# Loading a side job's first weights before the last projection, with rooms of their own and waits by tile

## The chip, the cores and the metric

The kernel runs on one NeuronCore of a Trainium2 chip. The metric is the device time of one execution in microseconds; of several runs the median counts. The profile comes from one further execution that was recorded; its times count from the start of its span.

## What is computed

One layer of a streaming encoder, on 1024 tokens of width 1024: a mixer with two groups of heads, a cross attention to 256 memory tokens, and an MLP, each added to its input.

```python
h = h + parallel_mixer(rms_norm(h, norm_mix_g), w_in, ..., w_out)
h = h + memory_cross_attention(rms_norm(h, norm_xattn_g), rms_norm(mem, norm_mem_g), xattn_wq, xattn_wkv, ..., xattn_wo)
u = relu(rms_norm(h, norm_mlp_g) @ mlp_w1)
h = h + (u * u) @ mlp_w2
```

Inside the mixer `proj = xn @ w_in` is split into queries, keys and values of 8 "forgetting attention" (FoX) heads and of 4 heads of gated linear attention (GLA). The two head groups' outputs stand side by side, and `w_out` projects them: rows 0 to 511 of `w_out` belong to FoX, rows 512 to 1023 to GLA. Memory keys and values are `memn @ wkv`; the keys are normalized and multiplied by the norm vectors.

## The kernel before

Every float32 product is made of three matmuls on split operands: each operand is a high part (rounded) and a low part (the rest), and `gemm` (lines 110 to 112) adds high·high, high·low and low·high. Splitting costs one instruction on ScalarE (the high part) and one on VectorE (the low part) for each tile of 128 x 512. `wsplit` does so for weights: it loads two blocks of 128 rows at a time into a tile `raw` (512 KB, line 80), and makes `wh` (line 88 or 99) and `wl` (line 93 or 100) of each block. There are nine rooms for such pairs; a tenth pair waits until the matmuls that read the first have ended. The `raw` tiles come by turns from a pool `rawp` with two rooms and, where `rooms` is given, from two rooms called `raw0` in that pool.

The order of the work on each engine is fixed when the program is built: a scheduler with a model of the durations places each instruction, and the engine then runs its own list in that order, waiting where an operand is not ready. ScalarE, VectorE and the queue of DMA issues on SyncE (SP) thus each hold up all that stands behind a waiting instruction. A memory room that a pool takes over from an earlier pool makes its first users wait for the last users of what lay there.

`mixer_inputs` computes the projections. Its last stages are, for each of 8 blocks of 128 tokens, the GLA output, and then the projection of the FoX values with W_FV: eight products of 24 matmuls (`token_major`), each evicted from PSUM by a pair on ScalarE and VectorE into a staging tile `qn` (lines 120 and 121), and written to DRAM as `vd` (line 596). While that runs, `fox_prep` loads queries and keys of the first heads (lines 636 to 642) and `fox_group` makes the first scores (lines 656 to 659), their maximum `nm` (661), exponential `p` (664) and normalization (667, on GpSimd).

Then comes `fox`: for each of 8 heads it loads the values `va` of all token blocks from `vd` (line 721), transposes `p` (`tr`, line 696), splits it (`pth`, `ptl`), and multiplies by the values (`pv`, lines 703 and 704). `va` needs all eight writes of `vd`. Between these steps a generator, `side_work`, is advanced: it first loads the norm vectors `gx` and `gxk` (lines 739 to 741), then runs `out_part`: it splits rows 512 to 1023 of `w_out` (the first 512 columns) with `wsplit`, splits the GLA outputs `mixg` into `sh` and `sl` (lines 832, 833), multiplies, adds `x` (`t2k`, lines 805, 806) and writes `hpd` (807). After that it loads `memT` and `mem` into `memr` (749, 754), and projects the memory with four slices of `wkv`. All tiles of the side work come from one pool `side`, which lies where `mixer_inputs` had its normalized input (`xn`: tiles `xh0`, `xl0` for tokens 0 to 511, `xh1`, `xl1` for the others); it waits for that pool as a whole, and so does every pool of `fox`.

Of the kernel before, what the change touches and what calls it, by code (L numbers as in the profile page):

```python
# [17 lines left out]
F32 = mybir.dt.float32  # L18
F32R = mybir.dt.float32r
# [3 lines left out]
ALU = mybir.AluOpType  # L23
AX = mybir.AxisListType
PSUM = bass.MemoryType.PSUM
# [3 lines left out]
D = 1024  # L29
M = 256  # L30
P = 128
KT = D // P
NT = S // P
# [18 lines left out]
class Layer:  # L52
# [11 lines left out]
        return pool.tile(shape, dt, tag=tag, name=f"{tag}_{self.n}", **kw)  # L64


    def wsplit(self, src, gcols, N=512, lo_pool=0, hi_pool=False, steps=None, beside=None, rooms=None, nraw=2):


        nc = self.nc  # L70
        kt = src.shape[0] // P
        hs, ls = [], []
        for k0, n in steps or [(k, 2) for k in range(0, kt, 2)]:
            if beside is not None:
                beside(k0, n)
            self.nr += 1
            raw = (self.T(self.rawp, [P, 2, N], F32, "raw") if rooms is None or nraw == 2 and self.nr % 2
                   else self.T(rooms, [P, 2, N], F32, "raw0", bufs=nraw))
            eng = nc.scalar if beside is not None and k0 == 0 else nc.sync
            self.raw_load = eng.dma_start(raw[:, 0:n], src[k0 * P:(k0 + n) * P, :].rearrange("(k p) n -> p k n", p=P))  # L80
            for j in range(n):
                wp = self.wps[self.nw % len(self.wps)]
                self.nw += 1
                wh = self.T(wp, [P, N], F32R, "wh")
                wl = self.T(wp, [P, N], F32R, "wl")
                r = raw[:, j, :]
                if gcols is None:
                    nc.scalar.activation(wh, r, AF.Copy)
                    if lo_pool and (k0 + j) % lo_pool == 0:
                        for c in (slice(0, N // 2), slice(N // 2, N)):  # L90
                            nc.gpsimd.tensor_tensor(wl[:, c], r[:, c], f(wh[:, c]), ALU.subtract)
                    else:
                        nc.vector.tensor_tensor(wl, r, f(wh), ALU.subtract)
                else:
                    g = self.cols[:, gcols + k0 + j:gcols + k0 + j + 1]
                    if hi_pool:
                        nc.gpsimd.tensor_scalar(wh, r, g, 1.0, ALU.mult, ALU.mult)
                    else:
                        nc.scalar.activation(wh, r, AF.Identity, scale=g)
                    nc.vector.scalar_tensor_tensor(wl, r, g, f(wh), ALU.mult, ALU.subtract)  # L100
                hs.append(wh)
                ls.append(wl)
        return hs, ls
# [94 lines left out]
    def build(self):  # L198
        with ExitStack() as st:
            dram = self.open(st, "dram", space=DRAM)  # L200
            self.qd = self.T(dram, [8, 2, 64, S], F32, "qd")
            self.kd = self.T(dram, [8, 2, 64, S], F32, "kd")
            self.vd = self.T(dram, [P, 8, NT, P], F32, "vd")
            self.cq = self.T(dram, [8, 4, S], F32, "cq")
            self.ck = self.T(dram, [8, 4, S], F32, "ck")
            self.kTd = self.T(dram, [P, 2, KT, M], F32, "kTd")
            self.vmd = self.T(dram, [P, 2, 2, D], F32, "vmd")
            self.od = self.T(dram, [P, 2, 2, KT, 512], F32, "od")
            self.hpd = self.T(dram, [2, KT, P, 512], F32, "hpd")
            self.hd = self.T(dram, [P, KT, S], F32, "hd")  # L210
            self.fd = self.T(dram, [P, 2, 512], F32, "fd")
            self.ud = self.T(dram, [NQ, P, 8, 512], F32, "ud")
            self.consts(self.open(st, "const"))
            self.smallp = self.open(st, "small", 6)
            ws = st.enter_context(ExitStack())
            self.rawp = self.open(ws, "raw", 2)
            self.wps, self.nw = [self.open(ws, "w", 9)], 0
            lst = st.enter_context(ExitStack())
            with ExitStack() as mx:
                self.mixg = self.T(self.open(mx, "mixg"), [P, NT, 4, P], F32, "mixg")  # L220
                with ExitStack() as mm:
                    self.mm_stack = mm
                    self.mixer_inputs()
                    self.side = self.open(mx, "side")
                    self.mixf = self.T(self.open(mx, "mixf"), [P, NT, 4, P], F32, "mixf")
                    self.fox()

                self.mmp = self.open(lst, "mm3", 2, space=PSUM)
                self.trp = self.open(lst, "tr3", 2, space=PSUM)

                self.h = self.T(self.open(st, "h", side="right"), [P, KT, S], F32, "h")
                self.project_out()
            self.xattn()
# [38 lines left out]
    def mixer_inputs(self):  # L272
        nc = self.nc
        w_in = self.w_in
        with ExitStack() as st:
            xnp = self.open(st, "xn")
            xh, xl = [], []
            for i in range(2):
                xh.append(self.T(xnp, [P, KT, 512], F32R, f"xh{i}"))
                xl.append(self.T(xnp, [P, KT, 512], F32R, f"xl{i}"))  # L280
            stp = self.open(st, "stg", 2)
            trp = self.trp = self.open(st, "tr1", 2, space=PSUM)
            mst, gst = ExitStack(), ExitStack()
            mmp = self.open(mst, "mm1", 3, space=PSUM)
# [39 lines left out]
            with ExitStack() as s2:  # L324
# [14 lines left out]
                def factors(t):  # L339
# [10 lines left out]
                                steps=[(0, 1), (1, 1), (2, 2), (4, 2), (6, 2)], beside=columns(0), rooms=xp, nraw=5)  # L350
# [138 lines left out]
            beside = decays()  # L489
# [98 lines left out]
            self.fox_first = self.fox_prep(0)  # L588
            self.fox_p = self.fox_group(0, 0, self.fox_first)
            W = self.wsplit(w_in[:, W_FV:W_FV + 512], C_MIX)  # L590
            for t in range(NT):
                ps = token_major(t, W)
                vv = self.T(stp, [P, 8, 2, 64], F32R, "qn")
                v3 = ps.rearrange("p (h d) -> p h d", h=8)
                self.evac_split(vv[:, :, 0, :], vv[:, :, 1, :], v3, self.xr[:, t:t + 1])
                nc.sync.dma_start(self.vd[:, :, t, :], f(vv).rearrange("p h s d -> p h (s d)"))
# [22 lines left out]


    def fox_open(self):
        self.foxp = self.open(self.mm_stack, "fox", 2, side="right")
        self.fox3 = self.open(self.mm_stack, "fox3", 3, side="right")
        self.fox_s = self.open(self.mm_stack, "sps", 1, space=PSUM, side="right")
# [49 lines left out]
    def fox(self):  # L674
        nc = self.nc
        with ExitStack() as st:
            pt = self.open(st, "foxpt", 5)
            olp = self.open(st, "foxol", 3)
            mmp = self.open(st, "mm2", 1, space=PSUM)
            pvp = self.open(st, "pv2", 1, space=PSUM)  # L680
            trp = self.open(st, "tr2", 3, space=PSUM)

            def values(h, sb, pp, A):
                va = A[4]
# [45 lines left out]
            for _ in side:  # L730
                pass

    def side_work(self, mp, mmp, trp):


        nc = self.nc
        v2 = lambda ap: ap.rearrange("p (h d) -> p h d", h=2)
        gk = self.T(mp, [P, 256], F32, "gxk")
        nc.sync.dma_start(self.gx, self.xq_g.partition_broadcast(P))
        nc.sync.dma_start(gk, self.xk_g.partition_broadcast(P))  # L740
        nc.vector.scalar_tensor_tensor(self.gx, self.gx, 0.0625, gk, ALU.mult, ALU.mult)
        yield from self.out_part(mp, mmp, 0, ())

        mh, ml = ([self.T(mp, [P, 4, P], F32R, n, bufs=6) for _ in range(4)] for n in ("sh", "sl"))
        gm = self.cols[:, C_MEM:C_MEM + 8]
        for t in range(2):
            c1 = slice(t, t + 1)
            xt = self.T(mp, [P, 4, M], F32, "memr")
            nc.sync.dma_start(xt, self.memT[:, 4 * t:4 * t + 4, :])
            for j in range(4):  # L750
                k, c = 4 * t + j, slice(2 * (j % 2), 2 * (j % 2) + 2)
                self.evac_split(mh[k // 2][:, c, :], ml[k // 2][:, c, :], xt[:, j, :].rearrange("p (t s) -> p t s", t=2), gm[:, k:k + 1])
            xt = self.T(mp, [P, D], F32, "memr")
# [3 lines left out]
            nc.gpsimd.tensor_tensor(self.mr[:, c1], self.mv[:, c1], self.mhalf[:, 0:1], ALU.pow)  # L757
            yield
        for n in range(4):
            W = self.wsplit(self.wkv[:, n * 512:(n + 1) * 512], None, rooms=mp)  # L760
            for t in range(2):
                ps = self.T(mmp, [P, 512], F32, "mm")
                self.gemm(ps, *([m[k // 2][:, 2 * (k % 2) + t, :] for k in range(KT)] for m in (mh, ml)), *W)
                kv = self.T(mp, [P, 2, 512], F32R, "mkv", bufs=2)
# [23 lines left out]
    def out_part(self, mp, mmp, n, ks):  # L788
# [1 line left out]

        nc = self.nc
        cs = slice(n * 512, (n + 1) * 512)
        W = self.wsplit(self.w_out[512:1024, cs], None, rooms=mp)
        if ks:
            W = [a + b for a, b in zip(W, self.wsplit(self.w_out[ks[0] * P:(ks[-1] + 1) * P, cs], None, rooms=mp))]
        for half in range(2):
            A = self.split_half(mp, self.mixg, half, 6, range(4))
            if ks:
# [546 lines left out]
```

## Time and profile before

| | |
|---|---|
| time, median of 3 runs | 1450.64 us (1450.14 to 1451.19) |
| time of the profiled execution | 1454.34 us |
| its span | 1452.6 us |
| mean granted TensorE clock | 0.996 |
| TensorE matmul busy | 1427.7 us (98%) |
| VectorE busy | 948.6 us (65%) |
| ScalarE busy | 679.9 us (47%) |
| GpSimd busy | 397.1 us (27%) |

The time of an execution is the span and about 1.7 us around it. The last matmul of the value projection starts at 326.62 us; `fox` with its side work fills the time from there to about 559 us. In rows of a timeline the first number is the start, the second the duration, both in microseconds; what stands in brackets is how long the engine was idle before and which engine and operation ended that. "PEclk" in a table of windows is the clock that TensorE was granted, as a share of full speed.

### The profile page before, as it was taken

To read this page: it belongs to the slowest core of one execution; us is meant where nothing else is said; L and a number is where in the kernel's file an instruction comes from. 1 tells how busy PE (TensorE), PEld (TensorE's weight loads), DVE (VectorE), ACT (ScalarE), POOL (GpSimd) and SP (SyncE) were. 2 spreads that over 40 slices of the span, in tenths; PEclk is the share of its full clock that TensorE was granted. 3 is DMA by queue.
4 is the path that set the end of the run, shared out by engine and by line. 5 is a ranking of instruction groups with operands and counts; after the bars stand their busy time and mean duration, and the time that the engine had idled before them with its cause. 6 is when DMAs were issued, how large, how long until landed. Compare 5 with 4: busy or idle time off the path is not lost.

```text
span 1452.6 us, 19224 instructions
## 1 busy us (share of the span) xinstructions
PE 1427.7 (98%) x7068; PEld 1190.0 (82%) x7068; DVE 948.6 (65%) x1354; ACT 679.9 (47%) x1095; POOL 397.1 (27%) x404
## 2 busy tenths in 40 slices
PE   9999999998999999999999999999999999999998
PEld 7788788887888887888888878887888888888887
DVE  5366732428798776666644895636556968788796
ACT  4444341327678565455542364445546735335230
POOL 3235513312242223521212300000000542333454
PEclk9999999999999999999999999999999999999999
DMA  8435520268677642412474124444445835336353
GB/s 273 128 73 131 138 70 1 73 176 252 203 211 234 188 140 87 132 59 88 150 266 170 51 80 153 174 174 189 174 174 209 322 121 188 131 122 225 119 198 119
DMA packets 121166, 223.94 MB, mean 154 GB/s; under 512 B 8912, under 2 KB 54512, under 8 KB 118512
## 3 DMA queue, kind: packets, MB, share of 16 engines
q1 hardware_dynamic: 119776, 218.25, 46.5%
q10 hardware_dynamic: 1296, 4.46, 1.0%
q8 instruction: 56, 0.92, 0.3%
q14 instruction: 38, 0.31, 0.1%
HBM read 150.59 MB, written 72.09 MB: 153 GB/s over the span
## 4 chain that ended last, share of the span: by engine, by line
PE 71%; issue 16%; DMA 6%; DVE 3%; ACT 2%; POOL 1%; ACTq 0%; SPq 0%; DVEq 0%; POOLq 0%
PE mm L110 13%; PE mm L112 13%; PE mm L111 13%; PE my L111 5%; PE my L112 5%; PE my L110 5%; PE tr L111 2%; PE tr L112 2%; PE tr L110 2%; PE tr L696 2%; PE pv L703 1%; DMA xt<-in_x_dram 1%; DMA raw<-in_w_in_dram 1%; PE pv L704 1%; PE s L656 1%
## 5 line engine op out<-in xcount | busy, mean ns | idle before, releaser
L111 PE MATMUL my<-x,g 128*128 128x512 f32 x464 | 180.6, 389 | 1.3 <-DVE x L1076 1.3
L110 PE MATMUL my<-x,g 128*128 128x512 f32 x464 | 180.6, 390 | 0.4 <-ACT h L1281 0.4
L112 PE MATMUL my<-x,g 128*128 128x512 f32 x464 | 180.5, 389 | 0.0
L111 PE MATMUL mm<-wl,xh 128*128 128x512 f32 x320 | 126.5, 396 | 0.9 <-DVE wl L100 0.8
L110 PE MATMUL mm<-wh,xh 128*128 128x512 f32 x320 | 126.0, 397 | 1.0 <-DVE sq L307 1.0
L112 PE MATMUL mm<-wh,xl 128*128 128x512 f32 x320 | 125.9, 394 | 0.0
L1075 ACT ACTIVATE g<-s 128x1024 fp32r<-128x1024 f32 (+1 forms) x72 | 68.7, 962 | 105.0 <-PE my L112 39.1
L1076 DVE TENSOR_TENSOR g<-raw,g 128x512 fp32r<-128x512 f32 (+3 forms) x72 | 69.2, 964 | 67.6 <-ACT g L1075 67.4
L111 PEld LDWEIGHTS my<-x,g 128*128 128x128 f32 x464 | 87.1, 188 | 19.9 <-DVE x L1076 1.7
L1101 POOL TENSOR_TENSOR s<-raw 128x384 f32<-128x384 f32 (+1 forms) x20 | 25.8, 1291 | 282.7 <-DVE h L1196 213.8
L110 PEld LDWEIGHTS my<-x,g 128*128 128x128 f32 x464 | 87.1, 188 | 18.8 <-ACT h L1281 0.8
L1075 ACT ACTIVATE g<-raw 128x512 fp32r<-128x512 f32 (+3 forms) x72 | 55.5, 773 | 100.3 <-DMA raw<-in_mlp_w_dram 40.1
L112 PEld LDWEIGHTS my<-x,g 128*128 128x128 f32 x464 | 87.1, 188 | 17.9
L667 POOL TENSOR_SCALAR p<-p,rrec 128x128 f32<-128x128 f32 (+3 forms) x64 | 57.9, 907 | 159.2 <-DVE rrec L666 151.9
L1076 DVE TENSOR_TENSOR g<-s,g 128x1024 fp32r<-128x1024 f32 (+1 forms) x72 | 88.2, 1228 | 7.6 <-ACT g L1075 7.5
L1243 DVE TENSOR_TENSOR x<-x 128x1024 fp32r<-128x1024 f32 (+1 forms) x64 | 76.8, 1220 | 17.3 <-ACT x L1242 17.1
L110 PE MATMUL mm<-x,g 128*128 128x512 f32 x220 | 85.8, 390 | 0.0
L112 PE MATMUL mm<-x,g 128*128 128x512 f32 x220 | 85.7, 389 | 0.0
L111 PE MATMUL mm<-x,g 128*128 128x512 f32 x220 | 85.6, 389 | 0.0
L110 PE MATMUL tr<-x,g 128*128 128x512 f32 x212 | 82.5, 389 | 0.0
L111 PE MATMUL tr<-x,g 128*128 128x512 f32 x212 | 82.5, 389 | 0.0
L112 PE MATMUL tr<-x,g 128*128 128x512 f32 x212 | 82.5, 389 | 0.0
(318 smaller groups left out, 3739.2 us busy)
## 6 DMA issues: line engine op xcount, KB each, us to landing
ud<-h SPq DMA_DIRECT2D x32, 768.0 KB, 3.8
x<-ud SPq DMA_DIRECT2D x48, 512.0 KB, 5.3
raw<-in_mlp_w_dram SPq DMA_DIRECT2D x20, 1024.0 KB, 7.4
raw<-in_mlp_w_dram SPq DMA_DIRECT2D x16, 768.0 KB, 6.0
raw<-in_w_in_dram SPq DMA_DIRECT2D x23, 512.0 KB, 5.0
raw<-in_xattn_wkv_dram SPq DMA_DIRECT2D x16, 512.0 KB, 7.4
od<-o SPq DMA_DIRECT2D x32, 256.0 KB, 4.0
ud<-h SPq DMA_DIRECT2D x32, 256.0 KB, 2.8
```

Source lines behind the costliest of these rows:

```text
L110: mm(ps, lh[k], rh[k], start=start and k == 0, stop=False, **kw)
L111: mm(ps, lh[k], rl[k], start=False, stop=False, **kw)
L112: mm(ps, ll[k], rh[k], start=False, stop=stop and k == n - 1, **kw)
L656: nc.tensor.matmul(ps[:, c], qa[:, ts], ka[:, c], start=True, stop=False)
L667: nc.gpsimd.tensor_scalar(p[:, 0:n], p[:, 0:n], rr, 1.0, ALU.mult, ALU.mult)
L696: nc.tensor.transpose(o, pp[i][:, kb * P:(kb + 1) * P], self.ident)
L703: nc.tensor.matmul(pv, va[:, kb, :], th[:, js], start=kb == 0, stop=False)
L704: nc.tensor.matmul(pv, va[:, kb, :], tl[:, js], start=False, stop=kb == nb - 1)
L1075: self.nc.scalar.activation(hi, src, AF.Copy)
L1076: self.nc.vector.tensor_tensor(lo, src, f(hi), ALU.subtract)
L1101: eng.tensor_tensor(s[:, 0], raw[:, 3], raw[:, 2], ALU.add)
L1243: nc.vector.tensor_tensor(lo, f(lo), f(hi), ALU.subtract)
```

## The change

Four things are edited. The first two `raw` tiles of `w_out` and the two norm vectors are loaded, and the vectors multiplied, by a new function `side_first`, which is called before the products of the value projection; they and the side work's later `raw0` tiles lie in a new pool `sidew`, on the other side of the memory from `xn`. `memr` and `mkv` get a pool of their own, `side0`. The pools of `fox` and of the side work are opened with waits by tile: a room waits for the tiles that lay in it, not for the whole pool. The staging pool `stg` is placed ahead of `xn`, so that `side0` comes to lie on the staging and `side` on `xn`.

```diff
-    def wsplit(self, src, gcols, N=512, lo_pool=0, hi_pool=False, steps=None, beside=None, rooms=None, nraw=2):
+    def wsplit(self, src, gcols, N=512, lo_pool=0, hi_pool=False, steps=None, beside=None, rooms=None, nraw=2, raws=()):
...
-            self.nr += 1
-            raw = (self.T(self.rawp, [P, 2, N], F32, "raw") if rooms is None or nraw == 2 and self.nr % 2
-                   else self.T(rooms, [P, 2, N], F32, "raw0", bufs=nraw))
...
+            if raws:
+                raw = raws[k0 // 2]
+            else:
+                self.nr += 1
+                raw = (self.T(self.rawp, [P, 2, N], F32, "raw") if rooms is None or nraw == 2 and self.nr % 2
+                       else self.T(rooms, [P, 2, N], F32, "raw0", bufs=nraw))
...
-                    self.side = self.open(mx, "side")
-                    self.mixf = self.T(self.open(mx, "mixf"), [P, NT, 4, P], F32, "mixf")
+                    kw = dict(reuse_waits="tile")
+                    self.side0 = self.open(mx, "side0", **kw)
+                    self.side = self.open(mx, "side", **kw)
+                    self.mixf = self.T(self.open(mx, "mixf", **kw), [P, NT, 4, P], F32, "mixf")
...
+            stp = self.open(st, "stg", 2)
             xnp = self.open(st, "xn")
...
-            stp = self.open(st, "stg", 2)
...
             W = self.wsplit(w_in[:, W_FV:W_FV + 512], C_MIX)
+            self.side_first()
...
     def fox_open(self):
+        self.sidew = self.open(self.mm_stack, "sidew", 2, side="right")
...
-            pt = self.open(st, "foxpt", 5)
+            kw = dict(reuse_waits="tile")
+            pt = self.open(st, "foxpt", 5, **kw)
...
+    def side_first(self):
+        self.raws0 = []
+        for k in (0, 2):
+            raw = self.T(self.sidew, [P, 2, 512], F32, "raw0")
+            nc.sync.dma_start(raw, self.w_out[512 + k * P:512 + (k + 2) * P, 0:512].rearrange("(k p) n -> p k n", p=P))
+            self.raws0.append(raw)
+        gk = self.T(self.sidew, [P, 256], F32, "gxk", bufs=1)
         nc.sync.dma_start(self.gx, self.xq_g.partition_broadcast(P))
         nc.sync.dma_start(gk, self.xk_g.partition_broadcast(P))
         nc.vector.scalar_tensor_tensor(self.gx, self.gx, 0.0625, gk, ALU.mult, ALU.mult)
...
-        W = self.wsplit(self.w_out[512:1024, cs], None, rooms=mp)
+        W = self.wsplit(self.w_out[512:1024, cs], None, rooms=self.sidew, raws=() if ks else self.raws0)
```

The scheduler's order is the same before the value projection and after about two thirds of `fox`; between them it is another. Three places show it. In the names, the last number counts tiles, and the tile of the last token block is `qn_2754` before and `qn_2765` after.

The queue of DMA issues, at the end of the projections. Before, from the loads of W_FV on to the first write of `vd`:

```order
L80 DMA raw_2496<-in_w_in_dram 128x2x512
L80 DMA raw_2506<-in_w_in_dram 128x2x512
L80 DMA raw_2516<-in_w_in_dram 128x2x512
L80 DMA raw_2798<-in_w_out_dram 128x2x512
L80 DMA raw_3709<-in_xattn_wkv_dram 128x2x512
L596 DMA vd_59<-qn_2551 1024x1x128
```

With the change:

```order
L83 DMA raw_2499<-in_w_in_dram 128x2x512
L747 DMA raw_482_2529<-in_w_out_dram 128x2x512
L747 DMA raw_483_2531<-in_w_out_dram 128x2x512
L751 DMA gxk_2533<-in_xattn_k_norm_g_dram 128x256
L83 DMA raw_2509<-in_w_in_dram 128x2x512
L83 DMA raw_2519<-in_w_in_dram 128x2x512
L83 DMA raw_3715<-in_xattn_wkv_dram 128x2x512
L83 DMA raw_3735<-in_xattn_wkv_dram 128x2x512
L602 DMA vd_59<-qn_2562 1024x1x128
```

Both halves of `w_out` and the vector stand ahead of the last W_FV loads now, and the second and fourth `raw` of `wkv` behind them.

The same queue where the value projection ends. Before, from the next to last write of `vd` to the first load of `va`:

```order
L596 DMA vd_59<-qn_2725 1024x1x128
L740 DMA gxk_2784<-in_xattn_k_norm_g_dram 128x256
L80 DMA raw_500_2788<-in_w_out_dram 128x2x512
L805 DMA t2k_2837<-in_xT_dram 128x512
L805 DMA t2k_2884<-in_xT_dram 128x512
L596 DMA vd_59<-qn_2754 1024x1x128
L805 DMA t2k_2944<-in_xT_dram 128x512
L749 DMA memr_3540<-in_memT_dram 128x1024
L80 DMA raw_771_3699<-in_xattn_wkv_dram 128x2x512
L721 DMA va_2422<-vd_59 128x1024
```

With the change:

```order
L602 DMA vd_59<-qn_2736 1024x1x128
L83 DMA raw_771_3705<-in_xattn_wkv_dram 128x2x512
L83 DMA raw_781_3725<-in_xattn_wkv_dram 128x2x512
L822 DMA t2k_2843<-in_xT_dram 128x512
L822 DMA t2k_2890<-in_xT_dram 128x512
L822 DMA t2k_2950<-in_xT_dram 128x512
L83 DMA raw_851_3975<-in_xattn_wkv_dram 128x2x512
L83 DMA raw_3985<-in_xattn_wkv_dram 128x2x512
L602 DMA vd_59<-qn_2765 1024x1x128
L729 DMA va_2425<-vd_59 128x1024
```

Four loads of `wkv` and all three of `t2k` stand ahead of the last write of `vd` now; `gxk` and `w_out` are gone from here, and `memr` stands behind `va`.

VectorE at the same place. Before:

```order
L661 TENSOR_REDUCE nm_2478<-s_457_2472 128x1
L666 RECIPROCAL rrec_2483<-rsum_2481 128x1
L661 TENSOR_REDUCE nm_2952<-s_545_2948 128x1
L121 SCALAR_TENSOR_TENSOR qn_2754<-mm_2729,xr_82,qn_2754 128x8x64
L661 TENSOR_REDUCE nm_2966<-s_550_2960 128x1
L833 TENSOR_TENSOR sl_2809<-mixg_120,sh_2808 128x512
L741 SCALAR_TENSOR_TENSOR gx_105<-gx_105,gxk_2784 128x256
```

With the change:

```order
L668 TENSOR_REDUCE nm_2481<-s_457_2475 128x1
L96 TENSOR_TENSOR wl_2811<-raw_483_2531,wh_2810 128x512
L673 RECIPROCAL rrec_2486<-rsum_2484 128x1
L96 TENSOR_TENSOR wl_3708<-raw_771_3705,wh_3707 128x512
L668 TENSOR_REDUCE nm_2958<-s_545_2954 128x1
L96 TENSOR_TENSOR wl_3712<-raw_771_3705,wh_3711 128x512
L96 TENSOR_TENSOR wl_3718<-raw_3715,wh_3717 128x512
L668 TENSOR_REDUCE nm_2972<-s_550_2966 128x1
L96 TENSOR_TENSOR wl_3722<-raw_3715,wh_3721 128x512
L124 SCALAR_TENSOR_TENSOR qn_2765<-mm_2740,xr_82,qn_2765 128x8x64
L850 TENSOR_TENSOR sl_2815<-mixg_120,sh_2814 128x512
```

Four low parts of `wkv` weights and the maximum of the second score now stand ahead of the last eviction. On ScalarE the four matching `wh` copies (`wh_3707` to `wh_3721`, line 91) stand ahead of the last `qn` in the same way. On TensorE the first matmul of the side work, `mm_2830<-sh_2814,wh_2798`, now stands ahead of the first transposes of `fox`, and not behind them and the scores.

More of the change, by code (lines that the diff above doesn't have):

```diff
@@ L75, in wsplit @@
                 beside(k0, n)
-            self.nr += 1
-            raw = (self.T(self.rawp, [P, 2, N], F32, "raw") if rooms is None or nraw == 2 and self.nr % 2
-                   else self.T(rooms, [P, 2, N], F32, "raw0", bufs=nraw))
-            eng = nc.scalar if beside is not None and k0 == 0 else nc.sync
-            self.raw_load = eng.dma_start(raw[:, 0:n], src[k0 * P:(k0 + n) * P, :].rearrange("(k p) n -> p k n", p=P))
+            if raws:
[4 more added lines that the diff above has]
+                       else self.T(rooms, [P, 2, N], F32, "raw0", bufs=nraw))
+                eng = nc.scalar if beside is not None and k0 == 0 else nc.sync
+                self.raw_load = eng.dma_start(raw[:, 0:n], src[k0 * P:(k0 + n) * P, :].rearrange("(k p) n -> p k n", p=P))
             for j in range(n):
@@ L676, in fox @@
         with ExitStack() as st:
-            pt = self.open(st, "foxpt", 5)
[L678 to L681, printed above, removed]
+            kw = dict(reuse_waits="tile")
+            pt = self.open(st, "foxpt", 5, **kw)
+            olp = self.open(st, "foxol", 3, **kw)
+            mmp = self.open(st, "mm2", 1, space=PSUM, **kw)
+            pvp = self.open(st, "pv2", 1, space=PSUM, **kw)
+            trp = self.open(st, "tr2", 3, space=PSUM, **kw)
             def values(h, sb, pp, A):
@@ L731, in fox @@
                 pass
+    def side_first(self):
+        nc = self.nc
+        self.raws0 = []
[4 more added lines that the diff above has]
+        gk = self.T(self.sidew, [P, 256], F32, "gxk", bufs=1)
+        nc.sync.dma_start(self.gx, self.xq_g.partition_broadcast(P))
+        nc.sync.dma_start(gk, self.xk_g.partition_broadcast(P))
+        nc.vector.scalar_tensor_tensor(self.gx, self.gx, 0.0625, gk, ALU.mult, ALU.mult)
     def side_work(self, mp, mmp, trp):
@@ L747, in side_work @@
             c1 = slice(t, t + 1)
-            xt = self.T(mp, [P, 4, M], F32, "memr")
+            xt = self.T(self.side0, [P, 4, M], F32, "memr")
             nc.sync.dma_start(xt, self.memT[:, 4 * t:4 * t + 4, :])
@@ L752, in side_work @@
                 self.evac_split(mh[k // 2][:, c, :], ml[k // 2][:, c, :], xt[:, j, :].rearrange("p (t s) -> p t s", t=2), gm[:, k:k + 1])
-            xt = self.T(mp, [P, D], F32, "memr")
+            xt = self.T(self.side0, [P, D], F32, "memr")
             nc.sync.dma_start(xt, self.mem[t * P:(t + 1) * P, :])
@@ L759, in side_work @@
         for n in range(4):
-            W = self.wsplit(self.wkv[:, n * 512:(n + 1) * 512], None, rooms=mp)
+            W = self.wsplit(self.wkv[:, n * 512:(n + 1) * 512], None, rooms=self.sidew)
             for t in range(2):
@@ L763, in side_work @@
                 self.gemm(ps, *([m[k // 2][:, 2 * (k % 2) + t, :] for k in range(KT)] for m in (mh, ml)), *W)
-                kv = self.T(mp, [P, 2, 512], F32R, "mkv", bufs=2)
+                kv = self.T(self.side0, [P, 2, 512], F32R, "mkv", bufs=2)
                 if n >= 2:
@@ L792, in out_part @@
         cs = slice(n * 512, (n + 1) * 512)
-        W = self.wsplit(self.w_out[512:1024, cs], None, rooms=mp)
+        W = self.wsplit(self.w_out[512:1024, cs], None, rooms=self.sidew, raws=() if ks else self.raws0)
         if ks:
-            W = [a + b for a, b in zip(W, self.wsplit(self.w_out[ks[0] * P:(ks[-1] + 1) * P, cs], None, rooms=mp))]
+            W = [a + b for a, b in zip(W, self.wsplit(self.w_out[ks[0] * P:(ks[-1] + 1) * P, cs], None, rooms=self.sidew))]
         for half in range(2):
```

4 lines of the change are left out of this document (removed).

## The prediction

> **What bounds the kernel now.** I read the page's first block, then a table of windows of 3.41 us from the end of the projections on, then TensorE's timeline there, and from each of its waits went back through the engine it named.
>
> ```profile
> PE 1427.7 (98%) x7068; PEld 1190.0 (82%) x7068; DVE 948.6 (65%) x1354; ACT 679.9 (47%) x1095; POOL 397.1 (27%) x404
> ```
>
> TensorE bounds all but 25 us of the 1452.6 us span, so no edit that leaves its matmuls alone can give more than that. The windows show where part of it lies (columns: sum of PE busy, then PE with its count, PEld, DVE, ACT, POOL, granted clock, DMA share, GB/s).
>
> ```profile
> 328.57:331.98 3.41, 1.92 (x14) 1.53 (x14) 2.20 (x5) 3.41 (x8) 0.00 (x0) 1.00 0.76 187
> 331.98:335.40 3.42, 2.35 (x10) 1.17 (x8) 3.42 (x7) 2.52 (x6) 0.31 (x1) 1.00 1.09 376
> 335.40:338.81 3.41, 2.51 (x6) 2.03 (x7) 3.41 (x7) 2.38 (x6) 2.17 (x2) 0.50 1.05 385
> 338.81:342.22 3.41, 3.41 (x12) 2.79 (x12) 3.41 (x8) 2.19 (x4) 1.08 (x1) 0.50 1.04 395
> 369.53:372.94 3.41, 2.38 (x11) 1.55 (x9) 1.04 (x2) 2.69 (x6) 1.00 (x3) 1.00 0.15 38
> 533.37:536.78 3.41, 2.21 (x13) 1.41 (x12) 3.41 (x7) 3.39 (x9) 0.54 (x1) 1.00 0.70 246
> 536.78:540.20 3.42, 3.42 (x16) 3.13 (x16) 2.44 (x8) 1.86 (x5) 1.63 (x3) 0.50 0.44 130
> ```
>
> Between 328.57 and 338.81 TensorE is idle for 3.5 us, and from 335.40 to 342.22 it also runs at half clock. The change touches that stretch. TensorE's rows, with the load of values that ends it:
>
> ```profile
> 326.62 0.39 PE L112 MATMUL mm<-wh,xl 128*128 128x512 f32 x1
> 331.51 0.50 PE L656 MATMUL s<-ka,qa 128*128 128x512 f32 x1 [1.24 <-ACT p L664]
> 336.30 0.79 PE L112 MATMUL mm<-sh,wl 128*128 128x512 f32 x1 [1.53 <-DVE wl L93]
> 341.39 0.41 PE L703 MATMUL pv<-pth,va 128*128 128x256 f32 x1
> 343.46 0.66 PE L696 MATMUL tr<-ident,p 128*128 128x128 f32 x4 [0.45 <-POOL p L667]
> 341.05 0.29 PEld L703 LDWEIGHTS pv<-pth,va 128*128 128x128 f32 x1 [0.18 <-DMA va<-vd]
> ```
>
> The last row is PEld's: the first `pv` waited for `va`, 0.18 us at its weights. The two waits of TensorE ahead of it, 1.24 and 1.53, thus cost nothing: what they took would have been waited for at 341.05. The chain that sets 341.39 is another. It starts at the last matmul of the value projection:
>
> ```profile
> 327.09 0.69 ACT L120 ACTIVATE qn<-mm,xr 128x512 fp32r<-128x512 f32 x1 [1.79 <-issue]
> 327.94 0.74 DVE L121 SCALAR_TENSOR_TENSOR qn<-mm,xr,qn 128x512 fp32r<-128x512 f32 x1
> 327.04 0.36 SPq L740 DMA_DIRECT2D gxk<-in_xattn_k_norm_g_dram  x1
> 327.44 0.43 SPq L80 DMA_DIRECT2D raw<-in_w_out_dram  x1
> 329.19 0.53 SPq L596 DMA_DIRECT2D vd<-qn  x1
> 336.18 0.80 SPq L721 DMA_DIRECT2D va<-vd  x2
> SPq L721 <- DMA vd<-qn: 4.1, 1, 4.1
> ```
>
> Matmul to 327.0, eviction on ScalarE (327.09) and VectorE (to 328.68), last write of `vd` issued at 329.19; SP then waits for its landing (last row, from the waits of SP: 4.1 us) and issues `va` at 336.18, 7.0 us after the write; `va` is there at 341.05, 4.9 us later. The side work's loads share those 12 us: the DMA share in the windows is 0.76 to 1.09.
>
> **The change, part by part.** (1) The first `w_out` tiles and the norm vectors come before the value projection. Their waits now are:
>
> ```profile
> 333.35 2.19 ACT L88 ACTIVATE wh<-raw 128x512 fp32r<-128x512 f32 x4 [0.91 <-DMA raw<-in_w_out_dram]
> 339.74 2.19 ACT L88 ACTIVATE wh<-raw 128x512 fp32r<-128x512 f32 x4 [1.21 <-DMA raw<-in_xattn_wkv_dram]
> 331.48 0.43 DVE L741 SCALAR_TENSOR_TENSOR gx<-gx,gxk 128x256 f32<-128x256 f32 x1 [1.21 <-DMA gxk<-in_xattn_k_norm_g_dram]
> 335.57 1.28 DVE L93 TENSOR_TENSOR wl<-raw,wh 128x512 fp32r<-128x512 f32 x2
> ```
>
> The waits of 0.91 and 1.21 for `w_out` and `gxk` go, and with them TensorE's 1.53 for `wl`. None stands on the chain of `va`, so they give nothing by themselves. The same count of `wh` and `wl` runs earlier, at 0.55 and 0.64 each, one pair of them at about 274 and the others inside the value projection. A window of that stretch hides them:
>
> ```profile
> 324.00:326.00 2.00, 2.00 (x11) 1.62 (x10) 0.44 (x2) 0.99 (x2) 0.41 (x1) 1.00 0.52 150
> ```
>
> TensorE is busy without a gap, and VectorE 0.44 and ScalarE 0.99 of 2.00 us: no cost. The last load of W_FV is issued behind two of 512 KB more; its matmuls come some 20 us later.
>
> (2) The order that follows from it is what I hold to decide. The `sidew` room of the second `w_out` tile goes next to `raw_771` of `wkv`, whose load now stands ahead of the last `vd` write. It may be issued when the tile's last `wl` is made, behind the `nm` of the block before. From the neighbours on VectorE:
>
> ```profile
> 321.78 0.41 DVE L661 TENSOR_REDUCE nm<-s 128x1 f32<-128x256 f32 x1
> 327.46 0.56 DVE L661 TENSOR_REDUCE nm<-s 128x1 f32<-128x384 f32 x1 [1.96 <-PE s L659]
> 328.59 1.08 DVE L661 TENSOR_REDUCE nm<-s 128x1 f32<-128x896 f32 x1
> L80 SPq DMA_DIRECT2D raw<-in_xattn_wkv_dram x1: 368/368/368, 275.5 to 275.5; - x1
> DMA to landing us min/median/max: 3.9/3.9/3.9
> L80 SPq DMA_DIRECT2D raw<-in_xattn_wkv_dram x4: 368/384/401, 342.5 to 347.1; - x4
> DMA to landing us min/median/max: 8.0/8.0/8.0
> ```
>
> The `wl` takes the place behind the `nm` of 321.78 (to 322.19), with its 0.64 and a release of about 0.1 the load is issued at 323.0. The two pairs of rows on landings are its bounds: 3.9 us with little else in the queue, 8.0 us behind other loads of the same size. So `raw_771` lands between 326.9 and 331.0. Behind it on the queue stand two loads that wait for nothing of the kind, ahead of it only a `vd` write; I take 4.5 us, near the low row: 327.5. ScalarE has the four `wh` of `raw_771` and its neighbour ahead of the last eviction, and its last work before is a `p` that ended at 325.30:
>
> ```profile
> 325.11 0.19 ACT L664 ACTIVATION_READ_ACCUMULATOR p<-s,nm 128x1 f32 x1
> ```
>
> So it waits some 2 us, and makes the first `wh` at 327.5 to 328.1. VectorE then has four `wl` and two `nm` ahead of the last `qn`: 4 x 0.64, and 0.50 and 1.00 for the `nm` by their starts, 4.06 in all: 328.1 + 4.06 = 332.15. `qn` takes 0.74 to 332.9. SP's two further `wkv` loads wait for the same `wl`, and the `vd` write comes behind them, at 332.95. That is 3.75 us later than 329.19. ScalarE's part of the eviction is done at 327.5 + 2.19 + 0.69 = 330.4 and no bound.
>
> (3) The transfers. The write had 7.0 us to its landing with `w_out`, `t2k`, `memr` and `wkv` around it. With the change `w_out` and `gxk` are gone and all but the two last `wkv` loads (1 MB) are issued well ahead. Bounds: 7.0 us, and from the table of DMA issues the same kind of a tile, alone:
>
> ```profile
> vmd<-mkv SPq DMA_DIRECT2D x4, 512.0 KB, 3.5
> ```
>
> I take 4.2 us, close to the lower row, since at the write's issue little is in flight but those two: landed at 337.1. `va` had 4.9 us beside 376 to 395 GB/s of other traffic and cannot fall below 3.9 (the 512 KB load in the emptier queue); I take 4.1: 341.2, against 341.05 before. The term is +0.15 us. Its low end, with `raw_771` there before ScalarE asks for it: VectorE starts at 327.46 behind TensorE's score, `qn` is done at 331.6, write 331.65, then 2.5 us (an estimate for 256 KB, from the 3.5 of 512 KB) and 3.9: 338.1, that is -2.9. TensorE's own work ahead of `pv` is the same 12 products and as many scores; without the half clock it would be through at about 338.7, no earlier than that. High end: 331.0 for `raw_771` gives the write at 336.45; with the old 7.0 and 4.9, 348.3: +7.2.
>
> (4) Waits by tile and the staging order. The pools' first users wait for tiles, not for the pool. On ScalarE this is the row
>
> ```profile
> 327.68 3.22 ACT L832 ACTIVATE sh<-mixg 128x512 fp32r<-128x512 f32 x6
> ```
>
> It starts right behind the last eviction (327.09), and with the change it still stands behind it in ScalarE's order. Only the second half's `sh` could be freed sooner, and TensorE has no other user of them: nothing. The new order of pools adds no instruction. The wait of 0.45 for GpSimd's `p` at 343.46 I count as gone, since the score it is made of stands earlier on TensorE now: -0.45 (0 if not).
>
> (5) The memory. `memr` (own pool, its load behind `va`) had this wait:
>
> ```profile
> 370.20 1.06 ACT L136 ACTIVATE memr<-memr 128x1024 f32<-128x1024 f32 x1 [4.30 <-DMA memr<-in_mem_dram]
> PE tr L696 <- POOL mr L757: 1.0, 1, 1.0
> ```
>
> TensorE stood 1.0 us behind it. In the new order some 9 us of products stand between the load's release and the transposes that need it, against a landing of 3.9 to 8.0 us: covered, -1.0. If the landing is the long one, 0.
>
> Sum against the profiled execution: +0.15 - 0.45 - 1.0 = -1.3 us, 1453.0. The profiled execution took 1454.34, of which 1452.6 is span; the median of the runs is 1450.64, 3.7 us below it. I carry the difference over: 1449.3.
>
> **The rivals.** A (faster): `raw_771` lands by 325.8, so ScalarE doesn't wait. Its 3.9 us with an empty queue give 326.9, so the issue would have to come some 1 us sooner than I have it, or the transfers be the fast ones. Then `pv` starts at 338.3: -3.1 - 0.45 - 1.0 = -4.5 us, 1446.1; with the half-clock window at 536.78 gone too (3.42 us that need 1.7) 1444.4.
>
> B (slower): `raw_771` waits in a full queue and lands 8 us after issue, at 331.0; the eviction of the last value block, which has no need of it, stands behind it on ScalarE. Write +3.5 us against my sum, `va` at 344.7, and TensorE, idle more than before, gets one half-clock window more, +1.7: 1449.3 + 5.2 = 1454.5. It decides (1453.5) where the landing takes more than 7.0 us. Against it: those 8.0 us were measured behind three like loads issued within 4 us; here stands one `vd` write.
>
> C (does not do what it says): the stall is only renamed. TensorE waits for `va` in place of `wl`, and `memr` is as late as before: 1450.64 + 0.15 - 0.45 = 1450.3.
>
> D (the clock): the Trainium skill, "TensorE: Matmul & The Clock Gate", section "Part 1: The HAM clock gate", says that the clock is halved only after at least one idle window of some 3.4 us. Here the rows disagree: half clock at 335.40 follows windows with 1.92 and 2.35 us busy of 3.41, and at 536.78 one with 2.21, none idle. A window with 2.38 busy (369.53) was followed by full clock. So between about 2.2 and 2.4 us of busy time the rows decide either way. In my sum TensorE idles about 2.6 us before the side work's first product and about 2.5 before `pv`; by the rows a window at half clock just behind `pv` is possible, where every matmul counts: +1.7, 1451.0. By the page alone there would be none, and the sum stays 1449.3.
>
> **How the numbers follow.** My forecast with its neighbours C and D (0.45, 0.10 and 0.06) holds 0.61; A has 0.27, since the loads were moved ahead by tens of us and a landing 1 us sooner suffices; B 0.12. About 0.2%, 2.9 us, is what a measurement of this kernel can tell from no change: A is faster (below 1447.7), B slower (above 1453.5), the forecast, C and D within; with the ends of B and D spilling over, 0.27, 0.60 and 0.13. The range reaches to A at its smaller gain with a little of the other window, 1445.6, and to short of B, 1453.0. The likeliest case's own range is 1448.0 to 1451.5.
>
> **What the profile after would show.** ScalarE waits about 2 us at line 91 for `raw` of `wkv` near 327; the last `qn` on VectorE ends at 332.9, not 328.68; the last `vd` write is issued near 333, `va` is there near 341; TensorE waits for `sh`, and again 2 to 3 us for `va`; the waits for `gxk` and `w_out` are gone, and so is that for `mr`. I am wrong towards faster if `raw_771` is there by 325.8 or the write lands in under 3 us, towards slower if it lands after 331 or a half-clock window lies behind the first `pv`.

## The result and the profile after

The changed kernel took 1461.65 us (median of 5 runs, 1458.66 to 1463.86), the kernel before 1451.19 (5 runs, 1450.14 to 1454.85): the ratio is 1.006, 95% interval 1.0038 to 1.0083. It is slower, and the profiled execution (1461.65 us, span 1459.6) shows TensorE's matmuls as before, with more idle time and a lower clock: 0.993 against 0.996. Medians below take in every execution; one execution of the kernel before (2843.68 us) and one with the eviction first (2894.29 us) were slow ones and stand in no ratio or range.

The first block of the page:

```profile
PE 1430.1 (98%) x7068; PEld 1192.9 (82%) x7068; DVE 949.4 (65%) x1354; ACT 680.8 (47%) x1095; POOL 391.9 (27%) x404
```

TensorE's rows at the end of the value projection, at the first `pv`, and at a later one:

```profile
327.90 0.39 PE L115 MATMUL mm<-wh,xl 128*128 128x512 f32 x1
334.06 0.79 PE L113 MATMUL mm<-sh,wh 128*128 128x512 f32 x1 [4.41 <-ACT sh L849]
336.15 0.66 PE L704 MATMUL tr<-ident,p 128*128 128x128 f32 x2 [1.30 <-DVE qn L124]
345.90 0.36 PE L711 MATMUL pv<-pth,va 128*128 128x256 f32 x1 [2.23 <-DMA va<-vd]
454.04 0.36 PE L711 MATMUL pv<-pth,va 128*128 128x256 f32 x1 [1.91 <-DVE mixf L717]
454.67 0.38 PE L712 MATMUL pv<-ptl,va 128*128 128x256 f32 x1 [0.28 <-DVE ptl L121]
```

The first `pv` starts 18.0 us behind the last matmul of the value projection (345.90 - 327.90); before it was 14.8 (341.39 - 326.62). And a wait of 2.2 us near 454 us is new.

**The first place.** The rows of ScalarE, VectorE and SP that lead to that `pv`:

```profile
330.73 2.19 ACT L91 ACTIVATE wh<-raw 128x512 fp32r<-128x512 f32 x4 [4.06 <-DMA raw<-in_xattn_wkv_dram]
332.82 0.67 ACT L123 ACTIVATE qn<-mm,xr 128x512 fp32r<-128x512 f32 x1
331.39 0.69 DVE L96 TENSOR_TENSOR wl<-raw,wh 128x512 fp32r<-128x512 f32 x1 [4.53 <-ACT wh L91]
335.27 0.74 DVE L124 SCALAR_TENSOR_TENSOR qn<-mm,xr,qn 128x512 fp32r<-128x512 f32 x1
323.18 0.55 SPq L602 DMA_DIRECT2D vd<-qn  x1
324.10 2.58 SPq L83 DMA_DIRECT2D raw<-in_xattn_wkv_dram  x2
333.17 2.58 SPq L83 DMA_DIRECT2D raw<-in_xattn_wkv_dram  x2
336.04 0.53 SPq L602 DMA_DIRECT2D vd<-qn  x1
342.31 0.81 SPq L729 DMA_DIRECT2D va<-vd  x2
```

The time before the first of these loads was issued and while it was on its way (the last two columns are DMA share and GB/s); then the `vd` write issued ahead of it, with its size and its time from issue to landing, and the DMA packets from 323 to 326 us and from 327 to 331:

```profile
320.00:324.00 4.00, 4.00 (x20) 3.31 (x20) 1.77 (x4) 2.11 (x6) 0.89 (x2) 1.00 1.06 243
324.00:328.00 4.00, 4.00 (x21) 3.27 (x20) 2.41 (x6) 2.06 (x5) 1.39 (x2) 1.00 1.02 249
vd<-qn SPq DMA_DIRECT2D x1, 512.0 KB, 4.1
DMA packets 1690, 0.87 MB, mean 290 GB/s; under 512 B 25, under 2 KB 1685, under 8 KB 1690
DMA packets 447, 0.87 MB, mean 218 GB/s; under 512 B 22, under 2 KB 22, under 8 KB 447
```

`raw_771` of `wkv` is issued at 324.10 and there at 330.73, 6.6 us later; the DMA engines had no room then, at a share of 1.06 before its issue and 1.02 behind it. What filled them at first is the next to last `vd` write, issued 0.9 us ahead of it. That write moves pieces of 128 values (512 bytes), `raw` rows of 512 values (2 KB): from 323 to 326 us 1685 of 1690 packets are under 2 KB, from 327 to 331 only 22 of 447. So `raw_771` had hardly begun at 326 and took at most 4.7 us from there, with `raw_781` and `t2k` behind it. Until 330.73 ScalarE waits 4.06 us, with the last value eviction behind it in its order. The last `vd` write is issued 8.1 us behind the last value matmul (2.6 before).

**The second place.** ScalarE near 450 us:

```profile
447.88 0.63 ACT L120 ACTIVATE mkv<-t2k 128x512 fp32r<-128x512 f32 x1 [2.96 <-DMA kTd<-mkv]
448.42 3.74 ACT L91 ACTIVATE wh<-raw 128x512 fp32r<-128x512 f32 x7
452.18 0.38 ACT L714 ACTIVATE ol<-pv 64x256 f32<-64x256 f32 x1
452.58 1.57 ACT L120 ACTIVATE pth<-tr 128x512 fp32r<-128x512 f32 x3
```

`mkv` has two rooms. In the new order the tile made at 447.88 waits 2.96 us for the room of one that is still being written to `kTd`, and it and seven `wh` stand ahead of the `ol` and `pth` that TensorE needs. Before, the `wh` stood apart, with `ol` and `pth` between them, and nothing waited for `kTd`:

```profile
441.39 0.66 ACT L117 ACTIVATE mkv<-t2k 128x512 fp32r<-128x512 f32 x1
441.91 0.62 ACT L117 ACTIVATE pth<-tr 128x512 fp32r<-128x512 f32 x1
443.16 1.71 ACT L88 ACTIVATE wh<-raw 128x512 fp32r<-128x512 f32 x3
444.89 0.38 ACT L706 ACTIVATE ol<-pv 64x256 f32<-64x256 f32 x1
```

**The clock.** Windows of the changed kernel (columns as in the prediction):

```profile
346.00:349.40 3.40, 3.40 (x14) 2.92 (x15) 0.94 (x4) 1.94 (x5) 0.55 (x1) 0.53 1.04 330
455.60:458.40 2.80, 2.80 (x10) 2.22 (x8) 2.80 (x6) 2.34 (x6) 0.02 (x1) 0.50 0.95 345
```

Right behind each of the two waits, at 345.90 and at 454.67, TensorE works without a gap at half clock; each such window of 3.41 us loses 1.7. A third one, at 59 to 63 us, lies in a part whose order is as before.

For a table over all profiles I cut the time into windows of 0.1 us and add up TensorE's idle time and, where the clock was half, half of its busy time. Idle + clock loss in us: A from the last value matmul to the first `pv`, B from there to about 400 us, C from there to about 480, D from there to the end of `fox`. The second column is the time from that matmul to the `pv`, the last the span of the profiled execution.

| kernel | first `pv` behind | A | B | C | D | span |
|---|---|---|---|---|---|---|
| before | 14.8 | 3.7 + 2.6 | 1.6 + 0.4 | 0.2 + 0 | 4.2 + 1.7 | 1452.6 |
| before, second profile | 14.1 | 4.8 + 0 | 1.0 + 0 | 0.2 + 0 | 4.0 + 0 | 1447.0 |
| changed | 18.0 | 8.0 + 2.0 | 0 + 1.7 | 2.6 + 1.7 | 4.2 + 1.7 | 1459.6 |
| changed, second profile | 17.6 | 6.8 + 2.7 | 0 + 0 | 2.9 + 1.7 | 4.0 + 1.7 | 1454.1 |
| waits by pool | 17.5 | 6.2 + 3.2 | 0 + 0 | 1.8 + 0 | 4.2 + 1.7 | 1454.1 |
| vd write first | 15.8 | 2.0 + 1.7 | 0.7 + 0 | 1.8 + 0 | 6.0 + 4.5 | 1454.3 |
| three rooms | 14.0 | 5.1 + 0 | 0 + 2.9 | 0.2 + 0 | 6.1 + 3.4 | 1456.2 |
| staging back | 18.2 | 4.8 + 2.5 | 0.4 + 0 | 2.5 + 3.2 | 5.9 + 3.1 | 1458.8 |
| eviction first | 11.4 | 4.2 + 0 | 0 + 2.9 | 3.2 + 1.7 | 4.0 + 0 | 1453.4 |
| third mkv room | 18.3 | 7.9 + 2.3 | 0 + 1.7 | 0.4 + 0 | 4.0 + 0 | 1450.8 |
| both mended | 11.8 | 4.6 + 0 | 0.7 + 1.7 | 0 + 0 | 5.8 + 3.2 | 1450.6 |

For one order the idle times repeat within about 2 us, while the clock loss comes and goes. The three profiles of the changed kernel's order with two `mkv` rooms lose 9.5 to 10.0 in A and 1.8 to 4.6 in C, the two of before 4.8 to 6.2 and 0.2.

### The profile page after: what moved, and what is told of

Read it like the earlier page. It is cut to its first block, busy times and chain, and to the rows that moved or that the text cites. A ratio compares the mean times of both kernels' runs of the same rounds, so it can differ in the third digit from the quotient of the medians.

```text
span 1459.6 us, 19216 instructions
## 1 busy us (share of the span) xinstructions
PE 1430.1 (98%) x7068; PEld 1192.9 (82%) x7068; DVE 949.4 (65%) x1354; ACT 680.8 (47%) x1095; POOL 391.9 (27%) x404
## 4 chain that ended last, share of the span: by engine, by line
PE 83%; DMA 7%; DVE 5%; ACT 3%; issue 1%; POOL 1%; ACTq 0%; DVEq 0%; SPq 0%
PE mm L113 14%; PE mm L114 13%; PE mm L115 13%; PE my L114 7%; PE my L115 7%; PE my L113 7%; PE tr L114 3%; PE tr L113 3%; PE tr L115 3%; PE tr L704 2%; DMA xt<-in_x_dram 1%; PE pv L711 1%; PE pv L712 1%; DMA raw<-in_w_in_dram 1%; DVE wl L96 1%
## 5 line engine op out<-in xcount | busy, mean ns | idle before, releaser
L674 POOL TENSOR_SCALAR p<-p,rrec 128x128 f32<-128x128 f32 (+3 forms) x64 | 53.7, 842 | 161.9 <-DVE rrec L673 153.6
```

The lines of the kernel that those rows point to most:

```text
L674: nc.gpsimd.tensor_scalar(p[:, 0:n], p[:, 0:n], rr, 1.0, ALU.mult, ALU.mult)
```

## The experiments

Theory A: the last eviction, and so the `vd` write and `va`, is late because ScalarE waits for a `wkv` tile whose room was taken until 324 us; what is left over comes from the order further on. Rivals, with letters of their own in this section: the transfers alone (B), chance of the clock alone (C), and that side work moved forward is missing later (D). Kernels that were run together share their chip and the runs of the kernel before; medians are compared among these. The first four were run together, then the next four, then the last.

**The vd write first.** The last eviction pair and the write are kept, and the first slice of `wkv` is put behind them:

```diff
+                self.fv_last = ev + (nc.sync.dma_start(...).ins,)
...
+            with ExitStack() as behind:
+                for ins in self.fv_last if n == 0 else ():
+                    behind.enter_context(self.tc.issue_after(ins))
+                W = self.wsplit(self.wkv[:, n * 512:(n + 1) * 512], None, rooms=self.sidew)
```

> The changed kernel, with the loads and splits of the first wkv slice ordered behind the last value eviction and the last vd write on ScalarE, VectorE and SP. Theory A (the write is late because ScalarE waits for raw of wkv and because four wl and two wkv loads stand ahead of it): the last vd write is issued 2.5 to 4 us behind the last matmul of the value projection (before 2.6, changed 8.1), the first pv starts 11.5 to 15 us behind that matmul (before 14.8, changed 18.0), no half-clock window lies behind it, and the time falls by 4 to 5 us against the changed kernel, to 1456 to 1458; if the second wait near 454 us goes as well, to about 1453. Rival B (the transfers set it: the write and va take as long wherever they stand): the first pv stays 17 us or more behind, time within 1 us of 1461. Rival C (only a half-clock window more or less): the first pv is earlier, but the time moves by under 2 us.

Measured: 1453.65 us (12 runs) beside 1452.77 of the kernel before (23 runs), ratio 1.0 (0.9988 to 1.0013). Run beside it, the order of the changed kernel, in the experiment with waits by pool, took 1461.93. The loss of 9 us is all but gone. TensorE's wait near 450 us is gone as well in this order (the 1.8 us in C are mostly a wait of 1.48 us at 409.15), so these 8.3 us are not the price of the first place alone. SP's rows:

```profile
328.25 0.53 SPq L602 DMA_DIRECT2D vd<-qn  x1
332.24 1.03 SPq L729 DMA_DIRECT2D va<-vd  x2
```

The write is issued 2.1 us behind the last value matmul (326.16) and takes 4.0 to the issue of `va`. The first `pv` is 15.8 us behind, later than forecast: 24 matmuls of the side work stand ahead of it in place of 12, half clock fell on some of them, and no wait for `va` is left; A loses 3.8 us in place of 10. Rival B falls: the transfers were late since they started late, and the write, with no `wkv` load just ahead of it, took 4.0 us in place of 6.3. Rival C falls too. But D lost 10.5 us in place of 5.9.

**Three rooms.** The pool `sidew` gets a third `raw0` room, so that `raw_771` need not wait for `w_out`'s:

```diff
-        self.sidew = self.open(self.mm_stack, "sidew", 2, side="right")
+        self.sidew = self.open(self.mm_stack, "sidew", 3, side="right")
...
-                       else self.T(rooms, [P, 2, N], F32, "raw0", bufs=nraw))
+                       else self.T(rooms, [P, 2, N], F32, "raw0", bufs=3 if rooms is getattr(self,"sidew",0) else nraw))
```

> The changed kernel with three raw0 rooms in sidew, so that the wkv raw tile that ScalarE waited 4.1 us for has a room of its own and is loaded early. Theory A: that wait goes; the four wl stay ahead of the last eviction on VectorE, so the last vd write is issued about 4.5 to 5.5 us behind the last value matmul (changed 8.1), the first pv about 15 us behind it, and the time falls by about 3 to 4.5 us, to 1457 to 1458.5. If the wait of ScalarE were not part of the cause, the write stays 8 us behind and the time at 1461.

Measured: 1455.06 us (12 runs), ratio to before 1.0009 (0.9999 to 1.002), 6.9 us under the 1461.93 of the changed kernel's order. ScalarE's and SP's rows:

```profile
326.00 1.66 ACT L91 ACTIVATE wh<-raw 128x512 fp32r<-128x512 f32 x3
327.57 0.67 ACT L123 ACTIVATE qn<-mm,xr 128x512 fp32r<-128x512 f32 x1
330.21 0.52 SPq L602 DMA_DIRECT2D vd<-qn  x1
```

The `wh` follow without a wait, with the same splits ahead of the eviction as in the changed kernel (one of them earlier by a place), and the write is 3.3 us behind the last value matmul (326.91) and not 8.1. So the late room is the larger part of the delay, and the splits that stood ahead cost little once their data are there. The fall was larger than expected, because the wait near 450 us is gone as well in this order (C 0.2), and D again loses more (9.5).

**Waits by pool.** `kw = dict()` takes the waits by tile back, in the two places of the change and also in two later stages that had them before:

> The changed kernel without the waits by tile (all pools wait as a whole, as before); every engine's order is that of the changed kernel. Theory: these waits decide nothing, since sh stands behind the last eviction on ScalarE either way: time within 1.5 us of the changed kernel's 1461, first pv 18 us behind the last value matmul. Rival: the waits by tile are what gives the remaining gain, and without them the first products of the side work come later and the time rises by 2 us or more.

Measured: 1461.93 us (6 runs, 1455.86 to 1464.56), ratio to before 1.0049 (1.0031 to 1.0068), within the interval of the changed kernel's 1.006. The order of every engine is the same with and without the waits by tile; they decide nothing here. The order of the changed kernel comes from the other three edits.

**Staging back.** `stp` opened behind `xn` again:

> The changed kernel with the staging pool behind xn again, as before. The order ahead of the last eviction is the same, but memr is loaded ahead of the last two wkv tiles and the rest of fox is ordered otherwise. Theory A: the first pv is as late as in the changed kernel (17.5 to 19 us behind the last value matmul), and the second wait near 454 us, which comes from the order there, is gone or another: 1457 if it goes with its half-clock window (2.2 + 1.7 us), 1461 if not. Rival: the staging order is the cause of the late first pv, which then falls to 15 us.

Measured: 1459.18 us (6 runs), ratio 1.0035 (1.0021 to 1.0048). The first `pv` is 18.2 us behind, as in theory A: the staging order is not its cause. The wait near 450 us is gone, but others of 1.86 and 2.36 us with half clock took its place, and the median fell by 2.7 where 4 was expected for a clean removal. With six runs of each, the intervals of the two ratios overlap.

**Eviction first.** As the first experiment, with only ScalarE's and VectorE's pair in `fv_last`. This order ends `fox` as the kernel before does:

> The changed kernel with only the splits of the first wkv slice ordered behind the last value eviction, on ScalarE and VectorE; their loads stay where the scheduler puts them. The order of the last third of fox is that of the kernel before, unlike in the experiments with the vd write first and with three rooms, which ended fox with about 4 us more of idle and half-clock time. Theory A (a late eviction delays the first pv; what the two experiments gained there, their other order gave back at the end of fox): last vd write 2 to 3 us behind the last value matmul, first pv 11.5 to 14 us behind it, end of fox as before (about 6 us lost), time 2 to 4 us under the kernel before. Rival D (side work that fills the early wait is missing later, whatever the order): about as much is lost after the first pv as was gained ahead of it, time within 1.5 us of the kernel before.

Measured: 1455.35 us (12 runs) beside 1453.84 of before (29 runs), ratio 1.0014 (1.0003 to 1.0026); the changed kernel beside them took 1458.36. The first `pv` came 11.4 us behind the last value matmul, the earliest of all, and D is back at 4.0. Yet nothing is won on the kernel before:

```profile
337.63 0.55 PE L711 MATMUL pv<-pth,va 128*128 128x256 f32 x1 [3.12 <-DMA va<-vd]
444.80 0.63 ACT L120 ACTIVATE mkv<-t2k 128x512 fp32r<-128x512 f32 x1 [2.54 <-DMA kTd<-mkv]
447.35 0.36 PE L711 MATMUL pv<-pth,va 128*128 128x256 f32 x1 [0.69 <-DVE mixf L717]
451.01 0.63 ACT L120 ACTIVATE mkv<-t2k 128x512 fp32r<-128x512 f32 x1 [1.44 <-DMA kTd<-mkv]
469.60 0.44 PE L712 MATMUL pv<-ptl,va 128*128 128x256 f32 x1 [1.62 <-DVE ptl L121]
```

TensorE asks for `va` after 8 us and waits 3.12 for it, which half clock follows (B 2.9). ScalarE's waits for `kTd` are still there (2.54 and 1.44 us), but cost TensorE only about 1 us, near 447; most of C's 4.9 us is the wait of 1.62 us for `ptl` at 469.60 and the half clock behind it, and the chain back from there to 459.6 us holds no wait for `kTd`. Forecast A was wrong in the time, D in the mechanism: what was won before the `pv` went into waits of this order.

**A third mkv room.** `"mkv", bufs=3` in place of 2; no engine's order changes:

> The changed kernel with three rooms for mkv in place of two; every engine's order is that of the changed kernel. Theory A: ScalarE's wait of 3.0 us for the landing of kTd (its mkv tile takes the room of the one being written out), behind which wh, ol and pth stand, is what TensorE waits for near 454 us: with the third room it goes, with the half-clock window behind it where there is one, and the time falls by 1.5 to 4 us against the changed kernel run beside it; the first pv stays 17 to 18.5 us behind the last value matmul. Rival: TensorE waits there for the seven wh and wl, not for the landing; then the wait stays above 1 us and the time within 1 us.

Measured: 1454.01 us (12 runs, 1450.05 to 1456.14) beside 1458.36 for the changed kernel (12 runs, 1455.21 to 1461.47) and 1453.84 for before: 4.35 us less, ratio to before 1.0004 (0.9993 to 1.0015). ScalarE at that place:

```profile
441.44 0.66 ACT L120 ACTIVATE mkv<-t2k 128x512 fp32r<-128x512 f32 x1
441.96 3.77 ACT L91 ACTIVATE wh<-raw 128x512 fp32r<-128x512 f32 x7
445.90 0.38 ACT L714 ACTIVATE ol<-pv 64x256 f32<-64x256 f32 x1 [0.17 <-PE pv L712]
```

No wait for `kTd` is left, the seven `wh` stand where they stood, and now `ol` waits for TensorE and not TensorE for `ol`. This is the cleanest of the experiments, since the order is unchanged: the landing of `kTd` causes the second wait, and the wait with its half-clock window is worth about 4 us. Its first `pv` is as late as ever (18.3 us), and it is level with the kernel before on this chip; so what the delay of the first `pv` costs net of the gains is less than its 3.5 us (at most 2.2, by the upper end of the ratio's interval).

**Both kernels again.**

> The changed kernel once more, beside the others on their chip and with a second profile. If the half-clock windows (five places in the first profile, two in that of its twin with waits by pool, at 1461.65 and 1455.86 us) fall by chance: other places and a time between 1456 and 1464, with the same waits of TensorE. If they belong to the kernel: five places again and 1460 to 1463.

> The kernel before once more, for a second profile: the same waits of TensorE at the end of the value projection (3.4 to 4 us) and half-clock time there if it follows from them; elsewhere in other places if it falls by chance.

Measured: the changed kernel 1458.36 us (12 runs), ratio to before 1.0033 (1.0022 to 1.0044), and in its profile half clock at three places; the kernel before in its one execution 1448.74 us, with none while TensorE worked. Its row of spans and clocks:

```profile
core 0: 1447.0 us, clock 1.000
```

Its waits are those of the first profile (A idle 4.8 against 3.7), so the clock loss does in part fall by chance, and half clock at the first place is no property of the kernel before. On that chip the runs of before lie between 1450.06 and 1457.62. The loss by the change is certain, its size is not: 10.5, 9.2 (with waits by pool) and 4.5 us between the medians on three occasions, 8.7, 7.1 and 4.8 by the ratios.

**Both mended**, the eviction first and the third room:

> The changed kernel with both mendings: the first wkv slice's splits behind the last value eviction, and three rooms for mkv. The order up to about 440 us is that of the experiment with the eviction first, the rest of fox is ordered anew. Theory A with two causes that add up: first pv 11 to 13 us behind the last value matmul, no wait of over 1 us near 450 us, time 1 to 3 us under that experiment (1452.5 to 1454.5, with the kernel before at 1453 to 1454). It beats the kernel before by 2 us or more only if the end of fox is not made worse by its order; in the two experiments whose end was ordered anew it lost 4 us more there, and then the time is within 2 us of the kernel before. Rival: the waits hide one another, and the time stays at 1455.

Measured: 1454.49 us (12 runs) beside 1452.77 (17 runs), ratio 1.0012 (1.0001 to 1.0023). The first `pv` is 11.8 us behind, C is 0 + 0, and up to 480 us it loses 7.0 us, where the changed kernel lost 16 and 14 and the kernel before 8.4 and 5.9. D takes it back, 9.0 us against 4.0 to 5.9. The three largest of TensorE's waits there (time, count, longest):

```profile
PE tr L704 <- DVE rrec L673: 1.5, 1, 1.5
PE s L663 <- ACT p L671: 1.4, 2, 1.2
PE pv L711 <- ACT pth L120: 1.0, 2, 0.8
```

All four orders that differ at the end of `fox` (here, vd write first, three rooms, staging back) idle 5.8 to 6.1 us in D, all that keep it 4.0 to 4.2. No version here beats the kernel before. Whether the end is worse because side work is used up earlier or only because of its order is not settled; no run changed the one without the other.

## Why the prediction was wrong

The forecast was 1449.3, no change; the time was 10.5 us above that of before. By its steps:

- *What bounds the kernel, and the chain of `va`.* Right. The chain from the last value matmul over eviction, `vd` write and `va` sets the first `pv` before and after, and the `pv` comes sooner in the runs in which it starts sooner (11.4 to 15.8 us behind, and not 18.0).
- *(1) The early loads.* Right that the waits for `w_out` and `gxk` go. That this gives nothing by itself no run shows alone.
- *(2) "I take 4.5 us, near the low row."* This step failed. `raw_771` was issued about where I had it (3.8 us ahead of the last value matmul, forecast 3.6), but took 6.6 us, inside the bounds of 3.9 and 8.0 but nearer the high one. "Ahead of it only a `vd` write" put that write at nothing, and it filled the DMA engines until about 326 us; from there on the load took at most 4.7 us, about what I had for all of it. ScalarE waited 4.06 us in place of 2, and the write was issued 8.1 us behind the last value matmul in place of 6.3.
- *(3) The landings.* The write took 6.3 us to the issue of `va`, where I took 4.2 and before had 7.0: the last two `wkv` loads were issued just ahead of it, at 333.17 and after. `va` took 3.6, where I took 4.1. The term that I put at +0.15 measured +3.2 (18.0 - 14.8). Rival B of the prediction named this mechanism and its price of 5.2 us with the half-clock window; I gave it 0.12. The low end was wrong too: it took 2.5 us for a write of 256 KB, but the write is of 512 KB, and the fastest one measured here landed in 3.5.
- *(4) Waits by tile and staging.* Right that the waits by tile give nothing (waits by pool, same time and order), and the 0.45 for `p` is gone. That the staging order "adds no instruction" was true and not enough: it changes the order.
- *(5) `memr`.* No wait for `mr` is left, and B has no idle time in the changed kernel, against 1.6 before. But the second profile of before has no such wait either, so not all of this 1.0 is the change's.
- *Rival D.* The half-clock window behind the first `pv` came in the first profile (1.7 us at 346) and with the third `mkv` room, not in the second profile nor with waits by pool. The Trainium skill, "TensorE: Matmul & The Clock Gate", section "Part 1: The HAM clock gate", wants at least one idle window of some 3.4 us. This case's trace does not agree: the 2.23 us ahead of 345.90 are less, and in the 4.41 us ahead of 334.06 (idle from 329.65) the clock averages 0.64 from 332.00 to 334.00, so it fell to half near 332.56, 2.9 us into them.
- *What the sum left out.* This failed too. The order was read where the prediction spoke of it, up to the first `pv`. It changes on for another 100 us, and there the landing of `kTd` makes ScalarE hold up `ol` and `pth`: 2.2 us of wait and 1.7 us of clock in the first profile, 4.35 us between the medians of two kernels with one order. No term and no rival had it. On the chip where both were priced it is nearly the whole loss: 4.35 of 4.5 us between the medians, with the first `pv` as late as ever. How the larger losses on the other two occasions divide between the two places stays open.

Added up for the two profiles first shown: +3.2 for the first `pv`, +1.7 for half clock behind it less 0.4 that before had there, -0.45 and -1.0 as forecast, +2.2 and +1.7 near 454, and +1.3 that the changed kernel was late already when the value projection ended, by its half clock at 59 us. That makes 8.3; the spans differ by 7.0. The 1.3 left over I can't assign; the half-clock losses, taken as half of the busy time, may be too large.

## What to carry to other kernels

A load that is moved ahead into a room of its own frees its place, and a scheduler with a fixed order will fill it: look at which load now reuses that room, when the room comes free, which transfer is issued just ahead of that load, and what stands behind its first reader on each in-order engine. An order that changes must be read to the row where the two lists meet again, not to the place that the change is about; each tile with two rooms and a write to DRAM in between is a wait that another order can expose. And where the clock falls to half behind a wait, count the wait with that window (here 1.7 us) and compare medians of many runs, since one execution may have it and the next not.

## What was not expected of the hardware

Half clock followed idle times much shorter than one of its windows of 3.41 us. In the eleven profiles TensorE was idle for 2.0 us or more at a stretch 15 times between the first matmul and the end of `fox`, and each time half clock, in one to three windows of 3.41 us, began during the wait or within 1.6 us of its end: eight waits of 3.1 to 4.5 us and seven of 2.00 to 2.36. Between 1.4 and 1.9 us it went either way: 1.62 us ahead of 469.60 with the eviction first was followed by it, 1.90 us at 59 us in the kernel before was not. Several short waits in a row can do it too, as at 335 us in the first profile of before, and need not, as in the second.
